# A decoder layer on one core: attention values transposed between two sets of scores, a prefetch moved, and a softmax ordered behind another

## The chip, the cores and the metric

The kernel runs on one core of one Trainium2 chip. The metric is the device time of one execution in microseconds. Before the change three runs gave 714.68, 715.93 and 716.32 us; the median is 715.93. The profile is of one more execution.

## What is computed

One layer of a decoder, for 512 positions of width 1024 in float32. A conditioning vector scales and shifts the normalised input (adaLN); one wide projection then feeds two causal attentions beside each other: A, a sliding window of 128 with 8 query heads on 2 key/value heads and a learned sink, and B, differential attention with 4 heads, each of which subtracts one softmax map from another. Both outputs are projected, gated and merged, and a gated MLP with a short causal convolution follows. The part that this document touches is the two attentions:

```python
def reference(...):
    mod = cs @ w_ada[l] + b_ada[l]
    h = _rmsnorm(x, norm1_g[l]) * (1.0 + scale1) + shift1
    proj = h @ w_in[l]
    qa, ka, va, qd, kd, vd, ga, gd = jnp.split(proj, points, axis=-1)
    out_a = _sliding_window_attention(qa..., ka..., va..., swa_sinks[l], slopes_swa)
    out_d = _diff_attention(qd..., kd..., vd..., lam, lam_init, diff_subln_g[l], slopes_diff)
    merged = sigmoid(ga) * (out_a @ w_branch_swa[l]) + sigmoid(gd) * (out_d @ w_branch_diff[l])
    x = x + gate1 * (merged @ w_out[l])
    ...
# in _diff_attention, for one block of 128 queries:
        p = jax.nn.softmax(scores, axis=-1)
        a = p[:, :, 0] - lam * p[:, :, 1]
        return jnp.einsum('bhqs,bshe->bqhe', a.astype(v.dtype), v)
```

## The kernel before

Every product of float32 matrices is made of three matmuls: each operand is kept as a high part, rounded by ACT (ScalarE), and a low part, which DVE (VectorE) gets by subtraction. So whatever leaves PSUM or comes in as a weight costs one ACT copy and one DVE subtraction (`split`, `evac`: L115/L116 for weights, L430/L431 and L433/L434 for results). In names, `_h` and `_l` (or `h`, `l` at the end) are these two parts.

**The order on PE** (TensorE) is written by hand, as the Python runs. The attention steps are fixed, and between them `fill(n)` puts n steps of background work: one step is three matmuls on 512 columns (one of the 8 steps of a projection of 128 columns). The work comes from a list, `units`: first q, k and v of head 0 of B (columns 768, 1280 and 1792: the tiles `w768_0`, `w1280_0`, `w1792_0`), then those of head 1, later gates (`wga`) and branch projections (`wba`) and the next heads. `prefetch()` starts loads of weights until two are loaded ahead, and splits them. `fill` calls it when it takes a new unit and, once more, when its step counter `tick` is 7. From some step on, `fill` also starts the rows of adaLN (`ra` loads of 512 KB, eight `arow` multiply-add steps on DVE for each half row).

**The order on ACT, DVE and SP** (the queue that issues nearly all loads) is made by a scheduler by priority. `tc.high_priority` raises what stands in it; `tc.issue_after(x)` makes what stands in it come after instruction x.

**Buffers.** Raw weights have 4, their parts 3 each. PSUM banks: `t` (all transposes) has 2, which go round by the order of allocation: a transpose waits until the evacuation of the last tile but one in its tag is done; `s` (scores) has 3, `f` (projections) 2.

**Attention A** goes by four pairs of heads. `swa_scores` (L536) makes the scores (`sw`) of two query blocks at once; DVE masks them and takes the maximum (L563, `st`). `swa_softmax` (L568) takes the exponentials on ACT (L575, L578) and scales on DVE (L582, L583, L586). `swa_transpose` (L588) turns the probabilities (`tp`, L598) and evacuates them to `pTh` and `pTl`; each of its two calls takes two `t` banks. `swa_values` multiplies with the values `va`. `va` itself is turned once, by `turn_va` (L448): ACT copies the projection (L445, `vaT`), PE transposes it in four pieces to the bank `pva` (L451), and ACT and DVE evacuate it in two halves.

**Attention B** goes by 16 steps s: head h = s // 4 and query block n = s % 4, whose width is (n + 1) * 128. `diff_scores` makes the scores and masks them on DVE (L680, which also gives the maximum); blocks 0 and 1 of a head come together. `diff_softmax` (L686) scales the maximum (L692, `dmx`), takes two exponentials on ACT (L694) and combines the two maps on DVE in four instructions (L697 to L700; the last one's output `sd` is the result). `diff_transpose` turns it (`td`, L709), and `diff_values` multiplies with the head's values (`od`). The tile `qkv` of each head holds the parts of its queries, keys and values; the last come by way of a transpose too (`pv`, L644). After `od`, the sums of squares of the head's output go through `pss` (L732).

Of the kernel before, what the change touches and what calls it, by code (L numbers as in the profile page):

```python
# [11 lines left out]
ALU = mybir.AluOpType  # L12
# [15 lines left out]
HP = 100000  # L28
# [8 lines left out]
SWA_FILL = (2, 2, 5, 2, 2, 2, 2, 3)  # L37
# [16 lines left out]
def kernel(  # L54
# [22 lines left out]
    nc = tc.nc  # L77
# [21 lines left out]
    def tbank(name, shape=(P, S)):  # L99
        return bank("t", 2, list(shape), name)  # L100
# [326 lines left out]

    def evac(hi, lo, src, scale=None):
        if scale is None:
            nc.scalar.copy(hi, src)  # L430
            nc.vector.tensor_sub(lo, src, hi.bitcast(F32))  # L431
        else:
            nc.scalar.activation(hi, src, AF.Copy, scale=scale)  # L433
            nc.vector.scalar_tensor_tensor(lo, src, scale, hi.bitcast(F32), ALU.mult, ALU.subtract)  # L434
# [3 lines left out]
    def evac_q(i):  # L438
        evac(qa[:, i, 0], qa[:, i, 1], acc6[i], qsc[:, i : i + 1])
# [8 lines left out]
    def turn_va():  # L448
        pv = tbank("pva")
        for t in range(NT):  # L450
            nc.tensor.transpose(pv[:, t * P : (t + 1) * P], vT[:, t * P : (t + 1) * P], ident)  # L451
        pv3 = pv.rearrange("p (t d) -> p t d", t=NT)
        for a, cc in ((0, 0), (64, 192)):
            evac(va[:, 0, :, cc : cc + 64], va[:, 1, :, cc : cc + 64], pv3[:, :, a : a + 64])
# [33 lines left out]
    current, tick = [], [0]  # L488

    def prefetch():  # L490
        while units and len(loaded) < 2:
            load, run = units.pop(0)
            loaded.append((load(), run))

    def fill(n):
        for _ in range(n):
            if not current:
                prefetch()
                if loaded:
                    wts, run = loaded.pop(0)  # L500
                    current.append(run(wts))
                    if tick[0]:
                        prefetch()
            if tick[0] == 7:
                prefetch()
            if current:
                try:
                    next(current[0])
                except StopIteration:
                    current.clear()  # L510
            for e in list(later):
                e[0] -= 1
                if e[0] <= 0:
                    later.remove(e)
                    e[1]()
            tick[0] += 1
            if tick[0] >= ADA_START and tick[0] % ADA_EVERY == 0:
                next(ada, None)
# [17 lines left out]
    def swa_scores(i, n0):  # L536
        if n0 == 0:
            c = pairs[i] = Pair()
            c.mx, c.nm, c.lsum, c.es = (
                ap.tile([P, 2, NT], F32, tag=t, bufs=2, name=f"{t}{i}") for t in ("mx", "nm", "lsum", "es")  # L540
            )
            c.sb = [ap.tile([P, 2, P], F32, tag="st0", bufs=2, name=f"st{i}_0")]
            c.sb += [ap.tile([P, 2, 256], F32, tag="st", bufs=ST, name=f"st{i}_{n}") for n in range(1, NT)]
            c.pT = []
        c = pairs[i]
        sps = [sbank(f"sw{i}_{n0}_{j}", (P, 2, 256)) for j in range(2)]
        for n in (n0, n0 + 1):
            w = P if n == 0 else 2 * P
            k0 = max(0, n - 1) * P
            qs, ks = slice(n * P, (n + 1) * P), slice(k0, k0 + w)  # L550
            mm3_rows([
                (
                    sps[j][:, n - n0, :w],
                    [qa[64 * j : 64 * j + 64, i, b, qs] for b in range(2)],
                    [ka[64 * j : 64 * j + 64, b, ks] for b in range(2)],
                )
                for j in range(2)
            ])
        for n in (n0, n0 + 1):
            w = P if n == 0 else 2 * P  # L560
            for j in range(2):
                with tc.high_priority(offset=HP):
                    c.last = nc.vector.tensor_tensor_reduce(  # L563
                        c.sb[n][:, j, :w], sps[j][:, n - n0, :w], dsw[:, 256 - w : 256], 1.0, -3e38, ALU.add, ALU.max,
                        c.mx[:, j, n : n + 1],
                    )
# [21 lines left out]
    def swa_transpose(i, j):  # L588
        c = pairs[i]
        ph = ap.tile([P, 1024], F32R, tag="aTh", bufs=2, name=f"pTh{i}_{j}")  # L590
        pl = ap.tile([P, 1024], F32R, tag="aTl", bufs=2, name=f"pTl{i}_{j}")
        for b in range(2):
            wb = 512 if b == 0 else 384
            tp = tbank(f"tp{i}_{j}_{b}")
            for m in range(wb // P):
                kb, n = 2 * b + m // 2, 2 * b + m // 2 + m % 2
                off = (kb - max(0, n - 1)) * P
                nc.tensor.transpose(tp[:, m * P : (m + 1) * P], c.sb[n][:, j, off : off + P], ident)  # L598
            with tc.high_priority(offset=HP):
                evac(ph[:, b * 512 : b * 512 + wb], pl[:, b * 512 : b * 512 + wb], tp[:, :wb])  # L600
        c.pT.append((ph, pl))

    def swa_values(i):
# [80 lines left out]
            scored[s] = mx, pm  # L684

    def diff_softmax(s):  # L686
        with tc.high_priority(offset=HP):
            h, n = divmod(s, NT)
            slope = 2.0 ** (-2 * (h + 1))
            mx, pm = scored[s]  # L690
            lsum = ap.tile([P, 2], F32, tag="dls", bufs=3, name=f"dls{h}_{n}")
            nc.vector.tensor_scalar_mul(mx, mx, -slope)  # L692
            for m in range(2):
                nc.scalar.activation(  # L694
                    pm[m], pm[m], AF.Exp, bias=mx[:, m : m + 1], scale=slope, accum_out=lsum[:, m : m + 1]
                )
            nc.vector.reciprocal(lsum, lsum)  # L697
            nc.vector.tensor_mul(lsum[:, 1:2], lsum[:, 1:2], nlam)
            nc.vector.tensor_scalar_mul(pm[1], pm[1], lsum[:, 1:2])
            nc.vector.scalar_tensor_tensor(pm[0], pm[0], lsum[:, 0:1], pm[1], ALU.mult, ALU.add)  # L700
            probs[s] = pm[0]

    def diff_transpose(s):
# [46 lines left out]
    def ada_rows():  # L750
        for idx in range(4):
            for hf in range(2):
                c0 = (2 + idx) * D + hf * S
                ac = big.tile([P, S], F32, tag="sq2", name=f"arow{idx}{hf}")
                for k in range(0, KT, 2):
                    r = raw_tile([P, 2, S], f"ra{idx}{hf}_{k}")
                    nc.sync.dma_start(r, wada[k * P : (k + 2) * P, c0 : c0 + S].rearrange("(a p) n -> p a n", p=P))
                    with tc.high_priority(offset=HP // 2) if tick[0] > ADA_EASY else ExitStack():
                        for a in range(2):
                            cc = cs[:, k + a : k + a + 1]  # L760
                            if k + a == 0:
                                nc.vector.tensor_scalar_mul(ac, r[:, a], cc)
                            else:
                                nc.vector.scalar_tensor_tensor(ac, r[:, a], cc, ac, ALU.mult, ALU.add)  # L764
                    yield
                ah = big.tile([P, S], F32R, tag="g2b0", name=f"arh{idx}{hf}")
                al = big.tile([P, S], F32R, tag="g2b1", name=f"arl{idx}{hf}")
                split(ah, al, ac)
                after(ADA_LAG, lambda idx=idx, hf=hf, ac=ac, ah=ah, al=al: ada_spread(idx, hf, ac, ah, al))
# [35 lines left out]
        units.append((lambda: load_cols(win, COL_GA + j * P, f"wga{j}"), gate))  # L805
        units.append((load, branch))

    pairs, firsts, scored, probs, aTs = {}, {}, {}, {}, {}
    ada = ada_rows()
    add_head(0)  # L810
    add_head(1)
    fill(SWA_FILL[0])
    swa_scores(0, 0)
    with tc.issue_after(pairs[0].last.ins):
        fill(SWA_FILL[1])
        swa_scores(0, 2)
    with tc.issue_after(pairs[0].last.ins):
        swa_softmax(0)
        fill(1)
        evac_q(3)  # L820
        turn_va()
        fill(SWA_FILL[2] - 1)
    for i in range(SWA_PAIRS):
        more = i + 1 < SWA_PAIRS
        if more:
            swa_scores(i + 1, 0)
        fill(SWA_FILL[3])
        swa_transpose(i, 0)
        fill(SWA_FILL[4])
        swa_transpose(i, 1)  # L830
        if more:
            swa_scores(i + 1, 2)
        fill(SWA_FILL[5])
        if more:
            swa_softmax(i + 1)
        fill(SWA_FILL[6])
        swa_values(i)
        fill(SWA_FILL[7])
# [5 lines left out]
    for j in range(2):  # L844
        add_gate_a(j)
    diff_scores(0, 1)
    diff_softmax(0)
    diff_softmax(1)
    fill(DIFF_FILL[0])
    for s in range(4 * DIFF_HEADS):  # L850
        h, n = divmod(s, NT)
# [672 lines left out]
    e = cbuf[1][:, 1024:2048].rearrange("p (t n) -> p t n", n=S)  # L1524
# [269 lines left out]
```

## Time and profile before

| | us |
|---|---|
| median of three runs | 715.93 |
| the profiled execution | 716.59 |
| its span | 714.5 |
| PE busy | 688.4 (96%) |
| DVE busy | 588.5 (82%) |
| ACT busy | 384.2 (54%) |
| PE idle by window: 70 to 80 us | 2.09 |
| 80 to 92 us | 0.81 |
| 140 to 160 us | 1.10 |
| 190 to 230 us | 1.03 |
| DVE waits for ACT's exponentials of B (L697), 56 to 260 us | 5.2 in 7 waits |
| loads of `w` on SP, 512 KB: issue to landing | 3.9 |
| loads of `ra` on SP, 512 KB: issue to landing | 4.2 |

Times inside a profile are microseconds from the start of the span. The granted clock of PE is 0.993 in the mean. The windowed view gives each engine's busy time in a stretch; what is missing to the length of the stretch is idle. The list of waits gives, for an engine and line, the idle time just before its instructions and what ended it. A line of the timeline gives the start, the duration (of all of them, where several are taken together), engine, line, operation, output and inputs, and in brackets the idle time before. Durations overlap a little with the next start: the step from one start to the next is the better price of an instruction in a full queue.

### The profile page before, as it was taken

To read this page: it belongs to the slowest core of one execution; us is meant where nothing else is said; L and a number is where in the kernel's file an instruction comes from. 1 tells how busy PE (TensorE), PEld (TensorE's weight loads), DVE (VectorE), ACT (ScalarE), POOL (GpSimd) and SP (SyncE) were. 2 spreads that over 40 slices of the span, in tenths; PEclk is the share of its full clock that TensorE was granted. 3 is DMA by queue.
4 is the path that set the end of the run, shared out by engine and by line. 5 is a ranking of instruction groups with operands and counts; after the bars stand their busy time and mean duration, and the time that the engine had idled before them with its cause. 6 is when DMAs were issued, how large, how long until landed. Compare 5 with 4: busy or idle time off the path is not lost. (4 is left out here: it accounts for less than half of the span.)

```text
span 714.5 us, 11275 instructions
## 1 busy us (share of the span) xinstructions
PE 688.4 (96%) x4187; PEld 603.0 (84%) x4187; DVE 588.5 (82%) x1125; ACT 384.2 (54%) x677; POOL 84.4 (12%) x101
## 2 busy tenths in 40 slices
PE   5999899999999999999999999999999999999994
PEld 5777778777787888888879999999999999888884
DVE  5998978797986774865479899888889899979996
ACT  3646566455554233432258666555555666656664
POOL 4000000001000100000012021111111102540300
PEclk9999999999999999999999999999999999999998
DMA  9983522453553664737717598877789738996903
GB/s 307 293 264 96 173 64 83 148 163 102 151 159 105 225 196 140 235 118 210 232 59 148 153 201 203 191 185 217 190 199 229 164 123 233 182 203 194 160 0 119
DMA packets 115863, 121.82 MB, mean 170 GB/s; under 512 B 4415, under 2 KB 93280, under 8 KB 115808
## 3 DMA queue, kind: packets, MB, share of 16 engines
q1 hardware_dynamic: 96894, 95.09, 42.1%
q0 software_dynamic: 18720, 25.73, 21.2%
q8 instruction: 33, 0.54, 0.3%
q10 hardware_dynamic: 194, 0.28, 0.1%
q14 instruction: 22, 0.18, 0.1%
HBM read 118.97 MB, written 2.11 MB: 169 GB/s over the span
## 5 line engine op out<-in xcount | busy, mean ns | idle before, releaser
L1133 PE MATMUL up<-t,m_whi 128*128 128x256 f32 x528 | 96.1, 283 | 0.0
L1133 PEld LDWEIGHTS up<-t,m_whi 128*128 128x128 f32 x528 | 82.3, 192 | 0.0
L1133 PE MATMUL up<-t,m_wlo 128*128 128x256 f32 x264 | 74.7, 283 | 0.1
L1133 PE MATMUL up<-bh,p_wlo 128*128 128x256 f32 x232 | 65.7, 284 | 0.6 <-DVE p_wlo L1076 0.6
L1133 PE MATMUL up<-bh,p_whi 128*128 128x256 f32 x232 | 65.6, 283 | 0.0
L1133 PE MATMUL up<-bl,p_whi 128*128 128x256 f32 x232 | 65.6, 283 | 0.0
L1133 PEld LDWEIGHTS up<-t,m_wlo 128*128 128x128 f32 x264 | 50.6, 192 | 0.3 <-DVE m_wlo L1076 0.3
L1133 PEld LDWEIGHTS up<-bh,p_wlo 128*128 128x128 f32 x232 | 44.4, 192 | 1.1 <-DVE p_wlo L1076 1.1
L1133 PEld LDWEIGHTS up<-bh,p_whi 128*128 128x128 f32 x232 | 44.5, 192 | 0.0
L1133 PEld LDWEIGHTS up<-bl,p_whi 128*128 128x128 f32 x232 | 44.5, 192 | 0.0
L1044 POOL DMA_DIRECT2D s<-in_w_up_dram x21 | 27.2, 1385 | 143.0 <-DMA s<-in_w_up_dram 92.7
L764 DVE SCALAR_TENSOR_TENSOR arow<-ra,cs,arow 128x512 f32<-128x512 f32 x56 | 41.9, 748 | 1.4 <-DMA ra<-in_w_ada_dram 0.7
L1076 DVE TENSOR_TENSOR m_wlo<-s,m_whi 128x1024 fp32r<-128x1024 f32 x31 | 37.7, 1216 | 2.0 <-ACT m_whi L1072 2.0
L1072 ACT CAST m_whi<-s 128x1024 fp32r<-128x1024 f32 x31 | 32.5, 1047 | 9.3 <-DVE s L1066 5.9
L1133 PE MATMUL up<-t,p_whi 128*128 128x256 f32 x176 | 32.2, 283 | 0.0
L175 POOL TENSOR_TENSOR r<-ms,mhalf 128x1 f32<-128x1 f32 (+1 forms) x16 | 13.4, 838 | 144.7 <-DVE ms L173 77.2
L694 ACT ACTIVATE sd<-sd,dmx 128x128 f32<-128x128 f32 (+3 forms) x32 | 17.8, 556 | 22.0 <-DVE dmx L692 15.4
L777 POOL DMA_DIRECT2D mod_rows<-arow x8 | 4.3, 540 | 200.5 <-ACT arow L776 200.3
L1133 PEld LDWEIGHTS up<-t,p_whi 128*128 128x128 f32 x176 | 27.4, 192 | 0.2 <-issue 0.2
L1140 ACT ACTIVATE gT<-a,cv 128x512 f32<-128x512 f32 x22 | 17.7, 813 | 17.6 <-DVE a L1175 17.3
L1072 ACT CAST p_whi<-wa 128x1024 fp32r<-128x1024 f32 x18 | 18.7, 1042 | 12.0 <-PE up L1133 10.8
L1133 PE MATMUL up<-t,p_wlo 128*128 128x256 f32 x88 | 24.9, 283 | 0.0
(485 smaller groups left out, 2119.5 us busy)
## 6 DMA issues: line engine op xcount, KB each, us to landing
ra<-in_w_ada_dram SPq DMA_DIRECT2D x32, 512.0 KB, 4.2
wa<-in_w_up_dram SPq DMA_DIRECT2D x22, 512.0 KB, 4.6
s<-in_w_up_dram SPq DMA_DIRECT2D x21, 512.0 KB, 5.0
s<-in_w_up_dram POOLq DMA_DIRECT2D x21, 512.0 KB, 6.5
adaw<-in_w_ada_dram SPq DMA_DIRECT2D x16, 512.0 KB, 5.1
w<-in_w_in_dram SPq DMA_DIRECT2D x12, 512.0 KB, 3.9
a<-in_w_up_dram SPq DMA_DIRECT2D x11, 512.0 KB, 4.7
b<-in_w_down_dram SPq DMA_DIRECT2D x10, 512.0 KB, 3.9
```

The costliest lines, as they stand in the source:

```text
L175: nc.gpsimd.tensor_tensor(r0, ms, mhalf[:, :n], ALU.pow)
L694: nc.scalar.activation(pm[m], pm[m], AF.Exp, bias=mx[:, m : m + 1], scale=slope, accum_out=lsum[:, m : m + 1])
L764: nc.vector.scalar_tensor_tensor(ac, r[:, a], cc, ac, ALU.mult, ALU.add)
L777: nc.gpsimd.dma_start(mod_rows[idx : idx + 1, hf * S : (hf + 1) * S], row)
L1044: nc.gpsimd.dma_start(dst, upblock(*blk), accum_op=ALU.add)
L1072: nc.scalar.copy(W[J, name][0], R[J, SRC[name]])
L1076: nc.vector.tensor_sub(lo, R[J, SRC[name]], hi.bitcast(F32))
L1133: nc.tensor.matmul(o[u], w[:, k, cu], b[:, k], start=name in ("p1", "m5", "p2") and k == 0 and x == 0, stop=k == 3 and x == 2, skip_group_ ...
L1140: nc.scalar.activation(grow(j), av[J][:, u], AF.Identity, bias=cv[:, 66 + j : 67 + j], scale=cv[:, 44 + j : 45 + j])
```

## The change

Three things, in the part of the kernel that holds the attentions:

1. `turn_va()` stood behind the softmax of the first pair and the last query evacuation. It now stands inside the second fill, between the first two sets of scores of pair 0.
2. `fill` no longer calls `prefetch()` at `tick` 7. A call of `prefetch()` stands behind the first `swa_transpose`, under `issue_after` of the ACT copy with which that transpose's last evacuation begins. For this, `evac` returns its ACT instruction.
3. In `diff_softmax`, for block 1 of every head, everything comes after the second exponential and the last DVE step of block 0.

```diff
     def evac(hi, lo, src, scale=None):
         if scale is None:
-            nc.scalar.copy(hi, src)
+            ins = nc.scalar.copy(hi, src)
             nc.vector.tensor_sub(lo, src, hi.bitcast(F32))
+            return ins
...
                     if tick[0]:
                         prefetch()
-            if tick[0] == 7:
-                prefetch()
...
-                evac(ph[:, b * 512 : b * 512 + wb], pl[:, b * 512 : b * 512 + wb], tp[:, :wb])
+                c.turned = evac(ph[:, b * 512 : b * 512 + wb], pl[:, b * 512 : b * 512 + wb], tp[:, :wb])
...
     def diff_softmax(s):
-        with tc.high_priority(offset=HP):
+        with tc.high_priority(offset=HP), ExitStack() as order:
             h, n = divmod(s, NT)
+            if n == 1:
+                for e in ends[s - 1]:
+                    order.enter_context(tc.issue_after(e.ins))
...
             for m in range(2):
-                nc.scalar.activation(
+                exp = nc.scalar.activation(
                     pm[m], pm[m], AF.Exp, bias=mx[:, m : m + 1], scale=slope, accum_out=lsum[:, m : m + 1]
                 )
...
-            nc.vector.scalar_tensor_tensor(pm[0], pm[0], lsum[:, 0:1], pm[1], ALU.mult, ALU.add)
+            end = nc.vector.scalar_tensor_tensor(pm[0], pm[0], lsum[:, 0:1], pm[1], ALU.mult, ALU.add)
+            ends[s] = exp, end
...
     with tc.issue_after(pairs[0].last.ins):
-        fill(SWA_FILL[1])
+        fill(1)
+        turn_va()
+        fill(SWA_FILL[1] - 1)
         swa_scores(0, 2)
     with tc.issue_after(pairs[0].last.ins):
         swa_softmax(0)
         fill(1)
         evac_q(3)
-        turn_va()
         fill(SWA_FILL[2] - 1)
...
         swa_transpose(i, 0)
+        if i == 0:
+            with tc.issue_after(pairs[0].turned.ins):
+                prefetch()
         fill(SWA_FILL[4])
```

The fills are `SWA_FILL = (2, 2, 5, 2, 2, 2, 2, 3)`. All lines of the kernel after the first edit shift by up to six in the changed kernel.

More of the change, by code (lines that the diff above doesn't have):

```diff
@@ L806, in add_gate_a @@
         units.append((load, branch))
-    pairs, firsts, scored, probs, aTs = {}, {}, {}, {}, {}
+    pairs, firsts, scored, probs, aTs, ends = {}, {}, {}, {}, {}, {}
     ada = ada_rows()
```

## The prediction

> **What bounds the kernel now.** I read the busy row and the slices of the page first.
>
> ```profile
> PE 688.4 (96%) x4187; PEld 603.0 (84%) x4187; DVE 588.5 (82%) x1125; ACT 384.2 (54%) x677; POOL 84.4 (12%) x101
> PE   5999899999999999999999999999999999999994
> DVE  5998978797986774865479899888889899979996
> ```
>
> PE is busy for 688.4 of 714.5 us and its low slices are the first and the last. So only PE's idle time can be won, some 26 us, and most of that lies at the ends. After the region that is changed PE runs with hardly a gap (230 to 700 us: 467.44 of 470), so a shift of PE there reaches the end. The profiled execution took 716.59 us: 714.5 of span and 2.1 outside. It is 0.66 above the median of the runs (715.93); I sum against 716.59 and then take off 0.66.
>
> Next I read the waits of PE between 56 and 260 us, the whole stretch that the edits reach (line, releaser: us in total, times, longest), then the busy time by windows around the first stalls (window length, then PE, PEld, DVE).
>
> ```profile
> PE tp L598 <- DVE pTl L431: 2.9, 2, 2.1
> PE td L709 <- DVE sd L700: 1.8, 4, 1.1
> PE od L120 <- DVE aTl L431: 0.5, 1, 0.5
> ```
>
> ```profile
> 66.00:70.00 4.00, 4.00 (x25) 3.06 (x23) 4.00 (x15) 2.93 (x14) 0.00 (x0) 1.00 0.00 0
> 70.00:80.00 10.00, 7.91 (x57) 6.32 (x54) 9.78 (x34) 5.17 (x14) 0.00 (x0) 1.00 0.45 133
> 80.00:92.00 12.00, 11.19 (x73) 9.23 (x72) 11.89 (x37) 8.76 (x25) 0.00 (x0) 1.00 0.63 197
> 92.00:100.00 8.00, 8.00 (x59) 7.03 (x57) 5.34 (x20) 5.63 (x22) 0.00 (x0) 1.00 0.26 69
> ```
>
> All that these waits hold is 5.2 us. The 2.9 are two stalls, 2.09 at 74.76 and 0.81 at 91.68. The window from 70 to 80 shows their cause: PE has 2.1 us idle while DVE is busy for 9.78 of 10. From 66 to 92 DVE is idle for 0.33 us in all, so there DVE is the bound, and an edit gains by what it takes out of DVE, not by what PE waits for by name. From 92 PE is the bound again (8.00 of 8).
>
> **Part 1, the values of the window attention transposed earlier.** Nothing is added or removed. Four transposes move on PE ahead of the second set of scores: the scores come 0.44 us later, and so does their mask on DVE (66.12 for 65.68 in this row). The two subtractions of va leave the full stretch:
>
> ```profile
> 65.68 0.42 DVE L563 CUSTOM_DVE_ANT_0 st<-sw,dsw 128x256 f32<-128x256 f32 x1 [1.30 <-PE sw L126]
> 67.99 0.41 DVE L431 TENSOR_TENSOR va<-pva,va 128x256 fp32r<-128x256 f32 x1
> 74.62 0.42 DVE L431 TENSOR_TENSOR va<-pva,va 128x256 fp32r<-128x256 f32 x1
> ```
>
> They start 0.33 apart from what follows, so 0.66 leaves, and they go into the 1.30 that DVE idles ahead of the mask. The two t banks rotate differently too: the second transposes of the first pair waited for the subtraction pTl of the first (the 2.09); now they take va's bank and go at once. But the next transposes then want the bank that pTl frees. Walking DVE's new order with these durations: the masks end 0.44 later, less 0.33 for the va that went, and one arow step (0.67) now stands before the scaling L586. The scaling starts at 71.55 for 70.80 and the first pTl at 74.76 for 74.01. The 2.09 go and a wait of 0.8 comes at the third transposes; PE is then 0.8 ahead at 77.4, but DVE isn't, and by the stall at 91.68 I have DVE 0.5 ahead, with that stall at 1.07 for 0.81. I take **-0.5**. The ends are 0 (the 0.66 offset by the late masks) and -2.9 (both stalls gone); I take the row in which DVE is full, since it says what PE gets.
>
> **Part 2, the third prefetch.** At most two weights are kept loaded. At the place where the new call stands two already are (v of head 0 and q of head 1, since the ninth step of filling), so it loads nothing. What the removed call leaves is that v's weight loads one step later, and on SP it changes places with the first ra load: issued at 55.78, not before. With the 3.9 us of that slot's ra it lands at 59.7. ACT's cast of it (1.04 at 56.85) moves behind the first copies of queries and keys, to 60.4. Cost **0**: the 0.7 us between landing and use hide it. Gone, it is paid in full by the copies behind it on ACT and the scores that need them: with 6.1 us to landing (the longest load below), +1.5. SP's other issues keep their order.
>
> **Part 3, the second block's softmax behind the first's.** Block 1's exponentials on ACT and its five DVE steps now wait for block 0's last step. Queued behind them on DVE is what the scheduler ranks lower, and it fills the gap with other work, some of it before block 0's own last steps. Four heads:
>
> Head 0 (129 to 141 us): block 1 is ready about 1.2 us later, at 134.6; PE wants it at 137.8. Cost 0, at most 0.5 through the mask of block 2.
>
> Head 1: this is the 1.1 of the waits above. Before:
>
> ```profile
> 152.09 0.16 DVE L698 TENSOR_TENSOR dls<-dls,nlam 128x1 f32<-128x1 f32 x1
> 152.16 0.55 DVE L699 TENSOR_SCALAR sd<-sd,dls 128x128 f32<-128x128 f32 x2
> 152.62 0.75 DVE L700 SCALAR_TENSOR_TENSOR sd<-sd,dls,sd 128x128 f32<-128x128 f32 x2
> 154.79 1.23 DVE L116 TENSOR_TENSOR w_l<-w,w_h 128x1024 fp32r<-128x1024 f32 x1
> ```
>
> Block 0's end is the first of two at 152.62, done at 152.97. In the new order block 1's small steps go, but the weight's low part (1.14 to the next start, at 154.79 here) and one arow (0.67) come between the reciprocal and that end. Walked from 148.57: arow 0.67, ta 0.67, aTl 0.60, reciprocal 0.07, arow 0.67, product 0.06, w_l 1.14, scaling 0.23, arow 0.67, end 0.30: 153.65. Cost 153.65 - 152.97 = **+0.7** on a PE that already waits; -1.1 if the low part slipped behind.
>
> Head 2: the gate's weight wga now has its low part on DVE ahead of the mask of block 2 and of qkv's low part, whose end frees the bank that PE needs at 188.38 (the sums pss). Before, it came after both:
>
> ```profile
> 186.30 0.68 DVE L431 TENSOR_TENSOR qkv<-pv,qkv 128x512 fp32r<-128x512 f32 x1
> ...
> 188.27 1.23 DVE L116 TENSOR_TENSOR wga_l<-wga,wga_h 128x1024 fp32r<-128x1024 f32 x1 [0.64 <-ACT wga_h L115]
> ```
>
> ```profile
> 187.19 1.05 ACT L115 CAST wga_h<-wga 128x1024 fp32r<-128x1024 f32 x1 [3.31 <-DMA wga<-in_w_in_dram]
> ```
>
> ACT's cast waited 3.31 us for the load, issued at 181.09, and nobody minded. Now DVE stands behind that load. In the new order two arow steps come sooner, so the load is issued near 180.4. What it takes, for all eight of its kind:
>
> ```profile
> DMA to landing us min/median/max: 5.3/5.5/6.1
> ```
>
> At 5.5 it lands at 185.9; cast to low part 1.08, low part 1.16, and from the mask's start to the end of qkv's low part as now (184.61 to 186.98, 2.4): 190.5. PE comes at 188.38 plus the 0.2 carried from above, 188.6: stall 1.9, and I add 0.3 where the last block (0.24 of wait before) comes behind. Cost **+2.2**; +2.0 with 5.3, +2.8 with 6.1, and +0.6 with the 3.9 us of this kernel's w loads, the same 512 KB.
>
> The Trainium skill (DMA: Bandwidth & Descriptors, Latency and other measured facts, with Specifications) has a fixed cost of about 2 us and 358 GB/s from HBM; my estimate from these two is 3.5 us for 512 KB. The rows of wga (5.3 to 6.1) stand against it, and by it the term would be about +0.2 and the sum +0.4.
>
> Head 3: PE has slack for a block 1 that is 1 us later; 0, at most +0.3. After it the orders are the same.
>
> **Sum:** -0.5 + 0 + 0.7 + 2.2 = +2.4, so 716.59 + 2.4 = 719.0 for a profiled execution and **718.3 us** against the median. Its own range: part 1 from -1.0 to 0, the load from 5.3 to 6.1, heads 0 and 3 up to +0.3: 717.6 to 719.7.
>
> **The rivals.** A measurement of this kernel can tell about 0.2% (1.4 us) from no change.
> - *The load lands soon.* wga in 3.9 us, as the w loads: -0.5 + 0.7 + 0.6 = +0.8, **716.7**, no change that can be told. For it: the same size and queue. Against: eight of eight wga loads took 5.3 or more. The skill's figure above belongs to this case. Chance 0.20.
> - *Faster: the bank turn pays in full.* The two stalls of the first transposes, 2.9, vanish, because va's bank is free and DVE runs ahead; with the lower end of head 2: -2.9 + 0.7 + 0.6 = -1.6, **714.3**. It decides once DVE reaches the transposes at 91.68 more than 2 us sooner than now; DVE's 0.33 us of idle from 66 to 92 speaks against it, the size of the 2.09 for it. Chance 0.20.
> - *The prefetch doesn't do what it says, and hurts.* v's weight lands after 60.4, the queries and masks behind its cast slip by up to 1.5: **719.8**. Chance 0.07.
> - *Forecast*, 718.3: chance 0.53.
>
> Slower by over 0.2% is the forecast and the late prefetch, 0.60; within 0.2% the second case, 0.20; faster 0.20. The range of 714.2 to 719.9 reaches to the price of the faster case and just past the late prefetch, and leaves some 0.15 out.
>
> **What would show it.** Part 1: no wait of 2.09 at the second transposes, one of about 0.8 at the third, and the stall near 91 about 0.3 longer; wrong if both are gone. Part 2: ACT's cast of w after the query copies with no DMA wait. Head 1: PE's wait on the first td of about 1.8 with w_l ahead of L702's end. Head 2: a wait of pss for qkv's low part near 188 to 190, about 2 us, with DVE waiting for wga's cast behind the DMA just ahead; if it is under 0.6 the load was soon. What would overturn the forecast is DVE finishing other work of its backlog earlier than this walk in one order, with durations held, can see.

## The result and the profile after

The change makes the kernel slower by a little: 717.90 us (median of 14 runs) against 715.93 (14 runs), a ratio of 1.0028 with a 95% interval of 1.0015 to 1.0041, or 2.0 us (1.1 to 2.9). The forecast was 718.3, in a range of 714.2 to 719.9; for a profiled execution it was 719.0.

The profiled execution of the changed kernel took 716.38 us, less than that of before (716.59) and less than most of its own runs (715.57 to 719.48). A second profile of each kernel, taken later (f2 and f3 below), took 715.84 and 714.72. So the two traces can't be compared by their ends. I read them from a point that both reach alike, the first scores of attention A (62.20 in before, 61.65 after), and follow how far PE has come at later points:

| from the first scores of A to | before | after | after - before |
|---|---|---|---|
| the first scores of B, head 0 | 62.84 | 62.12 | -0.72 |
| head 1's first transpose | 90.91 | 91.05 | +0.14 |
| head 1's last transpose | 110.64 | 110.48 | -0.16 |
| the sums of squares in head 2 | 126.18 | 126.63 | +0.45 |
| head 2's last transpose | 135.42 | 135.69 | +0.27 |
| head 3's last transpose | 159.61 | 161.43 | +1.82 |
| the sums of squares after it | 170.95 | 172.75 | +1.80 |
| the last matmul | 643.1 | 643.4 | +0.3 |

The attentions lose 1.8 us (1.2 between the second profiles, 172.75 for 171.56). The 1.5 that come back behind them are a wait of 1.3 in before, at the transposes of the second norm, which a second profile of the kernel before doesn't have; its stretch from the last sums of squares to the last matmul takes 470.64 us, and that of the change took 470.66.

First the waits of PE in the attentions of the changed kernel, in the form of the prediction's list:

```profile
PE tp L597 <- DVE pTl L431: 2.0, 2, 1.0
PE td L712 <- DVE dmx L694: 2.0, 1, 2.0
PE td L712 <- DVE sd L702: 1.7, 1, 1.7
PE pss L735 <- DVE qkv L431: 0.5, 1, 0.5
PE od L120 <- DVE aTl L431: 0.4, 1, 0.4
```

The 2.09 and 0.81 of attention A are now 1.00 and 0.96. In attention B the wait at head 1's first transpose is 1.96 for 1.10, the sums of squares (pss) have a wait that they did not have, and head 3's last transpose waits for 1.73 where it waited for 0.33:

```profile
221.81 0.63 PE L709 MATMUL td<-ident,sd 128*128 128x128 f32 x4 [0.33 <-DVE sd L700]
```

```profile
223.08 0.63 PE L712 MATMUL td<-ident,sd 128*128 128x128 f32 x4 [1.73 <-DVE sd L702]
```

The first row is of the kernel before, the second of the changed one. In the list of waits the releaser of the second line (`dmx`) is an instruction that stands right behind the one that PE needs (the list names the last that came before PE went on), so it is the same chain as in before. Now the window around the first waits, and the one that holds head 3's (length, PE, PEld, DVE, ACT, POOL, granted clock):

```profile
70.00:80.00 10.00, 9.00 (x55) 6.99 (x54) 10.00 (x38) 5.79 (x15) 0.00 (x0) 1.00 0.48 151
190.00:230.00 40.00, 37.83 (x197) 29.80 (x196) 31.28 (x81) 19.67 (x44) 2.51 (x3) 1.00 0.44 131
```

From 70 to 80 PE gained 1.1 us (9.00 for 7.91), and DVE, busy for 9.78 before, is now full. From 190 to 230 PE lost 1.1 (37.83 for 38.97).

### The profile page after: what moved, and what is told of

Read it like the earlier page. It is cut to its first block, busy times and chain, and to the rows that moved or that the text cites. A ratio compares the mean times of both kernels' runs of the same rounds, so it can differ in the third digit from the quotient of the medians.

```text
span 714.3 us, 11279 instructions
## 1 busy us (share of the span) xinstructions
PE 690.1 (97%) x4187; PEld 604.1 (85%) x4187; DVE 587.8 (82%) x1125; ACT 383.1 (54%) x677; POOL 83.3 (12%) x101
```

## The experiments

Each kernel was timed beside the kernel before. Waits are those of PE in us, from each kernel's profile (A is attention A, the heads are those of B); the ratio is to the kernel before in the same session, with its 95% interval. The ratio is the better measure: the kernel before had medians from 715.47 to 715.93 in the four sessions. e3 and e5 to e7 leave out the new `prefetch()` call, which is empty (below).

| run | what differs | median us | ratio | waits of PE |
|---|---|---|---|---|
| the change | all three edits | 717.90 | 1.0028 (1.0015 to 1.0041) | A 1.0, 1.0; head 1 1.96; head 2 0.5; head 3 1.7 |
| e1_values_prefetch | edits 1 and 2 | 713.59 | 0.9967 (0.9952 to 0.9983) | A 1.0, 1.0; head 1 1.1; head 3 0.3 |
| e8_values_only | edit 1 | 713.37 | 0.9977 (0.9967 to 0.9986) | as e1 |
| e4_prefetch_only | edit 2 | 715.84 | 0.9999 (0.9985 to 1.0013) | A 2.7; head 1 1.1 and 0.4; head 3 0.3 |
| e2_softmax_only | edit 3 | 718.67 | 1.0040 (1.0026 to 1.0053) | A 2.1, 0.8; head 1 2.0; head 2 0.4; head 3 1.7 |
| e3_sqrt_behind_mask | all, one DVE step moved | 716.99 | 1.0017 (1.0002 to 1.0032) | head 3 1.2, else as the change |
| e5_without_head1 | all but head 1 in edit 3 | 719.10 | 1.0047 (1.0031 to 1.0064) | A 1.0, 1.0; head 1 1.3 and 0.4; head 2 0.5; head 3 1.7 |
| e6_without_head2 | all but head 2 in edit 3 | 717.11 | 1.0027 (1.0014 to 1.0041) | A 1.0, 1.0; head 1 1.9; head 2's last transpose 0.6; head 3 1.7 |
| e7_without_head3 | all but head 3 in edit 3 | 715.99 | 1.0012 (1.0001 to 1.0023) | A 1.0, 1.0; head 1 1.9; head 2 0.5; head 3 0.3 |
| f1_rank_not_wait | edit 1, block 0 ranked higher | 713.68 | 0.9980 (0.9970 to 0.9991) | A 1.0, 1.0; head 1 0.8, its last transpose 0.6; head 3 0.6 |

### The three edits apart: e1, e2, e4, e8

e1 and e8 are the change without the ordered softmax; e8 also keeps the old prefetch:

```diff
 e1: diff_softmax as before; e8: this too
+            if tick[0] == 7:
+                prefetch()
```

> The first two edits without the ordered softmax. If the loss lies in the orders that the third edit makes (theory), this gains what the first edit won in the trace, about 0.8 us: near 715.1, with PE waits of about 1.0 at the third and the seventh transposes of attention A, and in attention B the waits of before (1.1, 0.2, 0.2, 0.3, 0.5). If the first edit wins nothing because the masks come later (rival), it is level with before, 715.9. If the slower kernel comes from the first two edits, it is above 717.

> The third edit alone. Theory: all of the loss and none of the gain, +2.0 to +2.8 against before, near 718.3, with PE waits of about 1.9 at head 1's first transpose, 0.5 at the sums of squares in head 2 and 1.7 at head 3's last transpose. Rival (the loss needs the shifted start of the first two edits, since it depends on when loads land): level with before, within 1 us.

> The second edit alone, which in effect starts one weight load a step later and behind the first load of the adaLN rows. Theory: nothing, 715.9, and no DMA wait of ACT before that weight's cast. Rival (the load lands after ACT wants it): up to 1.5 later, with that wait in the trace and the first scores later by as much.

> The first edit alone. The second edit alone made the wait at the second transposes 2.67 for 2.09, by one more weight or row step ahead on DVE. If that holds beside the first edit too (theory), the first edit alone wins 0.3 to 0.6 more than the two together: near 713.2. Rival (with va's bank free the order of that load no longer matters): 713.6, as the two together.

The loss is that of the third edit alone (e2: 1.0040), and the first edit wins (e8: 0.9977, e1: 0.9967). The ratios of e8, e4 and e2 multiply to 1.0016, at the lower end of the whole change's interval. The rivals of e1, e2 and e4 did not stand: edit 1 wins something, edit 3 needs no help of the other two, and the prefetch changes nothing that can be told (0.9985 to 1.0013). e1 won more than the 0.8 us that were expected. That e8 would win more than it, the theory of e8, was not borne out: in both the first scores of B come 0.7 to 0.8 sooner than in before (62.12 and 62.06), and the intervals of the times overlap. The trace of e1 shows edit 1 as the prediction had it, one wait split into two shorter ones:

```profile
PE tp L596 <- DVE pTl L431: 2.0, 2, 1.0
PE td L707 <- DVE sd L698: 1.6, 3, 1.1
PE od L120 <- DVE aTl L431: 0.5, 1, 0.5
```

From the first scores of A to the last sums of squares, e1 takes 169.81 us and e8 170.09, for 170.95 and 171.55 in the two profiles of before: 0.9 to 1.7 less, and the runs' medians are 2.1 less (the ratios say 1.6 and 2.4). The granted clock of their runs is higher too (below), which may be part of the difference.

Of edit 2 one half is empty. e3 leaves the new `prefetch()` call out, and its trace has the same instructions in the same order as the change on every engine and queue, but for the one DVE instruction that e3 moves. The other half, the removed call, moves one load. ACT's cast of it in the changed kernel:

```profile
59.16 0.70 ACT L434 ACTIVATE qa<-a,qsc 128x512 fp32r<-128x512 f32 x1
59.74 1.06 ACT L115 CAST w_h<-w 128x1024 fp32r<-128x1024 f32 x1
```

There is no idle time ahead of the cast, so the load had landed. In e4, with edit 2 alone, the wait of 2.09 is 2.67:

```profile
PE tp L596 <- DVE pTl L431: 2.7, 1, 2.7
```

### Which head loses: e5, e6, e7

```diff
-            if n == 1:
+            if n == 1 and h != 1:   # e5; h != 2 in e6; h < 3 in e7
```

> The whole change, but the third edit leaves head 1 as it was. Theory (each head's loss is its own, made by what the order puts ahead on DVE): the wait at head 1's first transpose falls from 1.96 to 1.1, heads 2 and 3 keep their 0.5 and 1.7, and the time falls by about 0.9 to near 717.0. Rival (the later heads' waits follow from head 1's delay): their waits go too and the time falls by 2 or more.

> The whole change, but the third edit leaves head 2 as it was. Theory: no wait at the sums of squares in head 2, heads 1 and 3 keep 1.96 and 1.7, the time falls by 0.2 to 0.5 to near 717.5. Rival (the gate's load, whatever ranks ahead, holds DVE in head 2): the wait of 0.5 stays.

> The whole change, but the third edit leaves head 3 as it was. Theory: the wait at head 3's last transpose falls from 1.7 to 0.4 and the time by 1.4 to near 716.5; that is more than the run with the reciprocal root behind the masks, since block 1's DVE steps then also go back into the gap of 0.8 ahead of the product with rb. Rival (head 3's wait comes from the delay of heads 1 and 2): it stays above 1.

In the traces head 3 is where most is lost. e7's attentions take 171.49 us for the change's 172.75. Its runs are 1.1 us below the change by the ratios and 1.9 by the medians, though the two intervals overlap. Head 3's last transpose waits in e7 for

```profile
PE td L711 <- DVE sd L701: 0.3, 1, 0.3
```

instead of 1.7, as expected. For heads 1 and 2 the theory of separate losses failed. Without head 1's order its wait is short again (the first transpose comes at 90.34 from the first scores, for 91.05), but at the sums of squares in head 2 only 0.2 of these 0.7 are left (126.45 for 126.63): behind head 1, DVE and the load in head 2 set the time, not PE. Without head 2's order its wait of 0.5 goes (125.99) and one of 0.58 comes at the head's last transpose (135.59 for 135.69). That wait need not come from the edit: in this execution the gate's weight took 6.5 us to land, and the kernel before, where it took 6.6 in its second profile (f3), has the same wait of 0.59; with 6.1, in its first, it was 0.24. So what is saved in head 1 is lost a few us later; that the same must happen to what is saved in head 2 is not shown. That e5's time is not below but above the change's was not expected; f4 shows a reason for one execution.

### What holds head 3 up: e3

In the changed kernel DVE goes through this ahead of the masks of head 3's last block:

```profile
214.46 0.16 DVE L171 TENSOR_SCALAR ms<-pss 128x4 f32<-128x4 f32 x1
214.54 0.61 DVE L702 SCALAR_TENSOR_TENSOR sd<-sd,dls,sd 128x384 f32<-128x384 f32 x1
216.07 0.16 DVE L183 TENSOR_TENSOR rt<-r 128x4 f32<-128x4 f32 x1 [0.93 <-POOL r L175]
216.15 0.75 DVE L767 SCALAR_TENSOR_TENSOR arow<-ra,cs,arow 128x512 f32<-128x512 f32 x1
216.82 0.68 DVE L679 CUSTOM_DVE_ANT_0 sd<-sd,ddf 128x512 f32<-128x512 f32 x1
```

L183 is a step on 128 x 4 numbers for the norm of head 2, which nobody needs soon. It waits 0.93 us for the reciprocal root on GpSimd, and the masks stand behind it. In before it came after them and found its input ready:

```profile
215.49 0.68 DVE L680 CUSTOM_DVE_ANT_0 sd<-sd,ddf 128x512 f32<-128x512 f32 x1
...
217.44 0.16 DVE L183 TENSOR_TENSOR rt<-r 128x4 f32<-128x4 f32 x1
```

e3 moves this one instruction back behind the masks and nothing else on any engine:

```diff
-            rstd_m2(rs, pss, NT, P, ap)
+            ms, r0 = rstd_start(pss, NT, P, ap)
+            def finish():
+                with tc.issue_after(masks[-1].ins):
+                    rstd_end(rs, ms, r0, NT, ap)
+            if h == 2:
+                after(1, finish)
+            else:
+                rstd_end(rs, ms, r0, NT, ap)
```

> The whole change, but in head 3 one DVE instruction, the first step after the reciprocal root from GpSimd (128 x 4), comes behind the two masks of the last block and not ahead of them; no other instruction moves on any engine. Theory (DVE stands behind GpSimd there for 0.9 us and the masks with it): the wait of 1.7 at head 3's last transpose falls to 0.3 to 0.5 and the time by 1.3, to near 716.6. Rival (it is the later block 1 that makes the last block late): the wait stays at 1.7 and the time at 717.9.

The wait fell, but to 1.2 and not to 0.3 to 0.5; the theory was half right. The trace of e3 shows the rest:

```profile
202.91 0.49 DVE L702 SCALAR_TENSOR_TENSOR sd<-sd,dls,sd 128x256 f32<-128x256 f32 x1
203.32 0.68 DVE L752 TENSOR_TENSOR of<-of,rb 128x512 f32<-128x512 f32 x1
...
215.40 0.75 DVE L776 SCALAR_TENSOR_TENSOR arow<-ra,cs,arow 128x512 f32<-128x512 f32 x1 [0.55 <-DMA ra<-in_w_ada_dram]
```

The row step that now stands first waits 0.55 for its load. And the end of block 1 (128 x 256, at 202.91) now precedes the product with rb. In before that product started after DVE had idled for 0.80, waiting for PE; block 1's steps were done before:

```profile
202.03 0.48 DVE L700 SCALAR_TENSOR_TENSOR sd<-sd,dls,sd 128x256 f32<-128x256 f32 x1
203.32 0.69 DVE L740 TENSOR_TENSOR of<-of,rb 128x512 f32<-128x512 f32 x1 [0.80 <-PE rb L739]
```

From the first scores it starts at 141.12 in before and at 141.86 in e3, where PE itself is only 0.2 later, and DVE carries the rest to the masks. So I read three things in head 3's loss: the root that DVE waits for, block 1's steps pushed out of a gap of DVE into a full stretch, and, once the root is out of the way, a load. e3 shows the first, at 0.55 us; the other two are read from its trace, and only e7, which undoes the order of head 3 as a whole, takes them away.

### A load that lands at different times: f2, f3, f4

e5's profiled execution took 715.27 us, and most of its timed runs 718.3 to 719.3. One more profile each was taken of the change, of the kernel before and of e5, with the kernels unchanged:

> The whole change, profiled once more. Theory: the same waits as in its first profile (1.0 twice, 1.96, 0.5, 1.7), the gate's load in head 2 landing in 3.7 to 4.0 us again, and the granted clock at half for about 3.4 us behind some of the waits of 1.7 or more, which is what differs between its executions. Rival (its executions differ by the landing of that load): it lands in 5 us or more, with a wait of 1.5 or more at the sums of squares in head 2.

> The kernel before, profiled once more. Theory: the same waits in the attentions (2.1, 0.8, 1.1, 0.2, 0.2, 0.3, 0.5); the wait of 1.3 at the transposes of the second norm, which no other profile has, is of that execution alone and goes; the clock may be at half behind the wait of 2.1.

> The whole change without head 1 in the third edit, profiled once more; its profile took 715.27 us and most of its timed runs 718.3 to 719.3. Theory: the clock at half behind a wait of 1.7 explains no more than 1.7 of these 4 us, so a wait that its first profile did not have must show, most likely the gate's load in head 2 landing late (5 us or more, for 3.7). Rival: nothing new shows, and the difference is left open.

The second profile of the change (715.84 us) has the waits of the first to within 0.1, and head 2's gate weight landed in 3.8 us, as in the first (3.7). That of before (714.72) has no wait at the second norm, as expected, but two of 0.6 at the last transposes of heads 2 and 3, so the attentions take 171.55 us instead of 170.95. Neither the half clock of the theory nor the rival's late load showed in the change, so what sets most of its timed runs above both of its profiles was not seen. Both showed in e5's second profile (718.37 us). There the load was issued at 178.73, as in the first (178.72), and landed in 5.3 us for 3.7 (first profile, then second):

```profile
wga<-in_w_in_dram SPq DMA_DIRECT2D x1, 512.0 KB, 3.7
```

```profile
wga<-in_w_in_dram SPq DMA_DIRECT2D x1, 512.0 KB, 5.3
```

ACT's cast and DVE's low part of the weight, then PE, in this second profile:

```profile
184.01 1.05 ACT L115 CAST wga_h<-wga 128x1024 fp32r<-128x1024 f32 x1 [2.98 <-DMA wga<-in_w_in_dram]
```

```profile
185.10 1.23 DVE L116 TENSOR_TENSOR wga_l<-wga,wga_h 128x1024 fp32r<-128x1024 f32 x1 [1.82 <-ACT wga_h L115]
186.24 0.55 DVE L678 CUSTOM_DVE_ANT_0 sd<-sd,ddf 128x384 f32<-128x384 f32 x1
...
187.93 0.68 DVE L431 TENSOR_TENSOR qkv<-pv,qkv 128x512 fp32r<-128x512 f32 x1
```

```profile
188.76 1.02 PE L734 MATMUL pss<-ones,sq 128*128 128x1 f32 x8 [1.98 <-DVE qkv L431]
```

This is head 2's mechanism as it was forecast, in its full size: ACT waits for the load, DVE for ACT, the mask and qkv's low part stand behind, and PE waits 1.98 us; with the load at 3.7 it waited 0.5. Against the first profile the sums of squares come 1.5 later (127.98 for 126.45), and 1.6 more are lost right behind, up to the next scores, where the granted clock is at half: together the 3.1 us between the two executions. Whether most of e5's timed runs had a late load too was not seen.

Over all fourteen profiles the landing of this load goes with the order of head 2. In the seven that have the third edit there it took 3.6 to 3.8 us six times and 5.3 once; in the seven that have the order of before, 4.3 to 6.6.

### The granted clock behind a wait

In three profiles the granted clock is at half for some 3.4 us, starting 1 to 2 us behind a long wait of PE. e2 behind its wait of 1.96 at head 1, then f4 behind its 1.98 (windows; the clock is the third number from the end):

```profile
153.00:154.00 1.00, 0.87 (x5) 0.76 (x6) 0.96 (x3) 0.84 (x3) 0.00 (x0) 1.00 0.65 147
154.00:155.00 1.00, 1.00 (x5) 0.99 (x4) 1.00 (x5) 0.40 (x3) 0.00 (x0) 0.56 0.94 340
155.00:156.00 1.00, 1.00 (x8) 1.00 (x6) 1.00 (x3) 0.00 (x0) 0.00 (x0) 0.50 1.06 327
156.00:157.00 1.00, 1.00 (x4) 0.81 (x4) 0.81 (x2) 0.79 (x2) 0.00 (x0) 0.50 1.15 345
157.00:158.00 1.00, 1.00 (x5) 0.82 (x4) 0.07 (x1) 0.90 (x2) 0.00 (x0) 0.73 1.15 345
```

```profile
190.00:191.00 1.00, 1.00 (x7) 0.59 (x6) 0.50 (x2) 1.00 (x2) 0.93 (x1) 0.87 0.48 115
191.00:192.00 1.00, 1.00 (x4) 0.71 (x3) 0.86 (x3) 0.62 (x2) 0.10 (x1) 0.50 0.90 315
192.00:193.00 1.00, 1.00 (x4) 0.81 (x3) 1.00 (x5) 0.00 (x0) 0.00 (x0) 0.50 0.25 94
193.00:194.00 1.00, 1.00 (x3) 0.79 (x3) 1.00 (x6) 0.17 (x1) 0.00 (x0) 0.50 0.00 0
```

PE is busy throughout and slow. In e2, from head 1's first transpose to the next scores it takes 6.49 us for 4.90 in before: 1.6 lost. In e4 the same happened behind the wait of 2.67. Behind other waits of 1.7 to 2.1 (both profiles of the change, both of before) the clock stayed up: in the attentions of all fourteen profiles 3 of 17 waits of 1.7 us or more were followed by such a stretch. Six profiles (before, the change, e2, e4, e6, f1) have another one at 14 to 15 us, ahead of all that the edits touch. Every timed run has a mean granted clock, and it goes with the number of waits of 1.7 us or more in the kernel's trace:

| waits of 1.7 us or more | kernels | mean granted clock |
|---|---|---|
| none | e8, e1, f1 | 0.9953, 0.9947, 0.9944 |
| one | before (63 runs), e7, e3, e5, e4 | 0.9938, 0.9938, 0.9932, 0.9930, 0.9924 |
| two or three | e6, the change, e2 | 0.9931, 0.9917, 0.9920 |

A stretch of 3.4 us at half clock lowers the mean of 715 us by 0.0024. The step from a row to the next is about half of that, as if about every second such wait were followed by one, which is more than the 3 of 17 in the profiles. That the waits cause the stretches is read from three traces and this table, and is not shown; no run here put a wait in for the purpose. So how the 2.0 us of the timed runs divide between longer waits and a lower clock stays open. The Trainium skill (TensorE: Matmul & The Clock Gate, What's actually happening) has the clock halved after an idle window of about 3.4 us that runs freely, without regard to the kernel. The length agrees with 3.4 us here; the stretches came behind idle times of 2.0 and 2.7 us, shorter than such a window.

### A rank in place of a wait: f1

```diff
 def diff_softmax(s):
-        with tc.high_priority(offset=HP):
+        with tc.high_priority(offset=2 * HP if s % NT == 0 else HP):
```

> The first edit alone, and block 0's softmax ranked above block 1's by a higher priority in place of a wait: block 0's last DVE step comes two places sooner, block 1's steps and everything else follow as DVE is free. Theory (a wait pushes block 1's steps out of DVE's gaps and pulls low-ranked work ahead; a rank does not): the wait at head 1's first transpose falls from 1.1 to 0.6 or less, no new wait in heads 2 and 3, and the time is that of the first edit alone or up to 0.6 less: 712.8 to 713.4. Rival (any reordering of these steps lets weights and rows ahead): waits over 0.5 in head 2 or 3, and 714 or more.

Head 1's wait fell to 0.8, not to 0.6. The waits at the last transposes of heads 1 and 3 are 0.6 each, for 0.2 and 0.3 in e8, and nothing is left of the gain: 713.68 and 713.37 us for f1 and e8. The second profile of before has waits of 0.6 as well, so one trace does not show that the rank made these. The theory's point on the order holds (no loss like the change's), its gain does not, and the rival's 714 or more did not come. The version to keep is the first edit alone or with the second, 0.2 to 0.3% faster than before; which of e1, e8 and f1 is best these runs don't tell.

## Why the prediction was right, and where it was wrong

- **The bound.** PE's idle time in the attentions decided, as read. From the first scores of A to the last sums of squares the traces take 169.8 (e1), 170.1 (e8), 170.5 (f1), 171.0 and 171.6 (before), 171.5 (e7), 172.2 (e3), 172.6 (e6) and 172.8 us (the change), and the ratios of the timed runs rise in nearly that order. e5 (172.6, but 175.6 in f4) and e4 (172.3) stand out. What the prediction left out is that a wait may be followed by a lower clock, as in e2, e4 and f4.
- **Part 1, -0.5.** Measured -0.72, and in the order that was walked: the 2.09 gone, 1.00 at the third transposes for a forecast 0.8, 0.96 at the seventh for 1.07. DVE was full from 70 to 80 (10.00 of 10), and the rival in which both waits go did not happen. In the runs the edit is worth 1.6 us by the ratio (e8), more than the walk gives; why is not shown.
- **Part 2, 0.** Right for the time: the new call is empty, the load landed in time, and alone the edit measured 0.9999. It did lengthen a wait, from 2.09 to 2.67 (e4), which was not forecast.
- **Head 0, 0.** Right; PE's distance is unchanged from its first scores to head 1.
- **Head 1, +0.7.** Measured +0.86 at its transpose, with the low part ahead of the end as walked. The lines of the changed kernel:

```profile
150.22 1.21 DVE L116 TENSOR_TENSOR w_l<-w,w_h 128x1024 fp32r<-128x1024 f32 x1
151.35 0.28 DVE L701 TENSOR_SCALAR sd<-sd,dls 128x128 f32<-128x128 f32 x1
151.55 0.74 DVE L767 SCALAR_TENSOR_TENSOR arow<-ra,cs,arow 128x512 f32<-128x512 f32 x1
152.21 0.34 DVE L702 SCALAR_TENSOR_TENSOR sd<-sd,dls,sd 128x128 f32<-128x128 f32 x1
```

  But the sum took it as carried to the end, and e5 shows that it isn't: 0.3 came back by the head's last transpose and only 0.2 of the saving reached head 2's sums.
- **Head 2, +2.2: the term of the sum that was mis-sized.** The mechanism was right and the load's time was not. It was taken as 5.5 us, with "eight of eight" loads at 5.3 or more. But the trace of before has a landing time for only three of the eight, 6.1, 5.5 and 5.3 us, and the line of minimum, median and maximum is of these three. The 6.1 is of this load, in the order that the edit changes. In the change it was issued when it was forecast to be (179.79, which is 118.1 from the first scores, as 180.4 is in before) and landed in 3.7 and 3.8 in the two profiles; the wait was 0.47 where 1.9 was forecast. The rival had this landing, and its row: the same 512 KB in 3.9 us. With 5.3 us, in f4, the wait was 1.98, where the walk gives 1.7. Why the load is sooner in the new order is open, and which landing the timed runs of the change had was not seen.
- **Head 3, "0, at most +0.3": wrong.** It lost 1.5 us (1.3 between the second profiles). The new order had the norm's step L183 ahead of the masks, and the walk counted it as one short step, not as a wait for GpSimd; nor was the gap of 0.80 that block 1's steps had filled looked for. e7 gives nearly all of it back (its stretch from head 2's last transpose to the last sums of squares is 35.61 us, for 35.52 in before and 37.06 in the change) and e3 a third (0.55 from the first scores to the last sums of squares).
- **The sum.** +2.4 forecast and +2.0 measured, but head 2 was 1.7 too dear in the trace and head 3 1.5 too cheap. In the traces the size came out by two errors that cancel, and that is luck; the direction came from the order in heads 1 to 3, and the runs bear that out (e2).

## What to carry to other kernels

A wait that is put on a block of work to get another ahead does more than delay it: lower-ranked work is then put ahead of it, and each such instruction brings its own waits (a load, another engine) in front of work that is on the path. Read the new order for instructions that wait, not only for long ones, and ask which gap the delayed steps had filled. Price a transfer by what stands beside it at its new place, not by the rows of its old place, and look how many rows a median is made of. A PE wait of 2 us may cost more than 2 us: three of 17 here were followed by a stretch at half clock.

## What the runs showed of the hardware

- Half the granted clock for about 3.4 us behind PE waits of 1.96, 1.98 and 2.67 us (e2, f4, e4), at 1.6 us of lost time in e2; 14 other waits of 1.7 to 2.1 us had none behind them.
- The same load of 512 KB from the same place in the same kernel took 3.7 us in one execution and 5.3 in another, issued within 0.01 us of the same moment; over all profiles this load took 3.6 to 6.6.
- A round trip from DVE to GpSimd and back for 128 x 4 numbers took 1.6 us in the changed kernel (214.46 to 216.07), of which the GpSimd instruction itself is 1.3.
